# Seven-product groups for the first token half of a feed-forward layer too

## The chip, the cores and the metric

The program runs on one core of a Trainium2 chip. The metric is the device time of one execution in microseconds; lower is better. The kernel before takes 2988.46 us, the median of 3 runs (2985.38 to 2988.88). PE is the matrix engine (TensorE), DVE the vector engine, ACT the scalar engine, POOL the general engine (GpSimd) and SP the engine that issues most of the transfers.

## The reference

One block of a diffusion transformer, on 2048 tokens of 1024 channels in fp32. The part after the state space scan, which is what the change touches, is this:

```
vb = silu(layernorm(depthwise_conv31(v * sigmoid(v2)) + dw_bias))
merged = sigmoid(g_a) * (ya @ w_proj_a) + sigmoid(g_b) * (vb @ w_proj_b)
x = x + g1 * (merged @ w_out)
h = rmsnorm(x, norm2_g) * (1 + sc2) + sh2
x = x + g2 * ((silu(h @ w_gate) * (h @ w_up)) @ w_down)      # hidden 2816
out = rmsnorm(x, norm_f_g)
```

The hidden width is 2816, which is 22 column tiles of 128. The convolution has 31 taps and runs over the tokens, channel by channel.

## The kernel before, in words

Matmuls at fp32 accuracy are made from three: each operand is split into a high and a low part (ACT writes the high part, DVE subtracts it to get the low part), and high·high, high·low and low·high are accumulated. A *product* here is four 128-row steps of contraction for 512 tokens of one column tile: 12 matmuls of 128x512.

The 2048 tokens go through the tail in two halves of 1024, one after the other. For the first half: `merge` (L1080), `out_proj` (L1099) in two pieces of 512 tokens, `h2` (L1124, the norm and modulation), `ffn` (L1148), `final` (L1599, transposes of the result, last norm, output). Then the same for the second half, whose `merge` begins beside the first half's `final`.

The two halves have different feed-forward code. The first half's `ffn` makes gate and up of a column tile by 96 matmuls (8 products for 1024 tokens and both matrices) and adds the down product to an accumulator in SBUF, by one DVE instruction per column tile of the result and chunk (L1191). The second half's `ffn_s` makes 20 of its 22 tiles in *groups* of seven products, 84 matmuls (`group`, L1415): it forms sums and differences of the weights on DVE (L1390 to L1397), uses sums of the activations that were prepared before, and puts the results together from PSUM by DVE and ACT (L1430, L1432, L1456, L1460, L1462). Its down product is scaled by ACT (L1526) and added to the array d_x1 in HBM by accumulating transfers that POOL issues (L1527). Its weights are staged as a list of jobs (`next_job`, L1358): converted three jobs ahead, sums formed five ahead, loaded seven ahead, with a ring of four raw tiles beside the pool's own two.

Background work is written as generators that are advanced from within the matmul loops. `tick` (L79) is called at every third matmul and adds a credit, RATE; a generator issues its next piece when there is credit, and `dve` subtracts what the foreground itself needs of DVE. `finish` (L112) issues whatever is left of a generator at once. The second half's convolution (`conv` L903: 29 DVE instructions per channel tile at L920, 232 in all; `conv_stat` L1024: the statistics, with 8 matmuls at L1047, a Newton iteration of 12 small DVE steps at L141 to L147, and `rstd_row`, whose matmuls at L973 each need a DVE tile from L971) runs in the background of the first half's `ffn`. `conv_apply` (L1056) follows it. `mod_rest` (DVE work at L347) is earlier background work beside the first half's `merge`.

Engines run their instructions in the order in which the program's scheduler puts them; tiles come from pools (16 slots each, four scratch buffers and two raw weight buffers and so on), and a tile waits for the last reader of the buffer it takes.

Of the kernel before, what the change touches and what calls it, by code (L numbers as in the profile page):

```python
# [28 lines left out]
RATE = (0.75, 0.65, 0.61, 0.53, 0.56)  # L29
# [11 lines left out]
GAP_L, GAP_V, GAP_R = 1440, 1792, 2016  # L41


class Kernel:
# [158 lines left out]
    def setup(self):  # L203
        tc, nc, A, ctx = self.tc, self.nc, self.A, self.ctx
        self.cp = ctx.enter_context(tc.tile_pool(name="const", bufs=1))
        self.small = ctx.enter_context(tc.tile_pool(name="small", bufs=2))
        self.gap("gapl", GAP_L)
# [694 lines left out]
    def conv(self, vp, ft, hf, csum):  # L902
# [3 lines left out]
        x = vp.tile([128, HALF + 30], F32, tag="cin", name=self.nm("cin"), bufs=2)  # L906
# [23 lines left out]
    def conv_edge(self, vp, csum):  # L930
# [3 lines left out]
        t = vp.tile([128, HALF + 30], F32, tag="cin", name=self.nm("edge"), bufs=2)  # L934
# [88 lines left out]
    def conv_stat(self, vp, hf, csum, res):  # L1023
# [10 lines left out]
        for k in range(8):  # L1034
            c = vp.tile([128, HALF + 30], F32, tag="cin", name=self.nm("cvs"), bufs=2)[:, 0:HALF]
# [19 lines left out]
    def conv_apply(self, vp, hf, S, st, res):  # L1055
# [4 lines left out]
        for k in range(8):  # L1060
            x = vp.tile([128, HALF + 30], F32, tag="cin", name=self.nm("cva"), bufs=2)[:, 0:HALF]
# [62 lines left out]
    def h2(self, hf, rs, S, res, c0=0, W=HALF):  # L1124
        nc = self.nc
        cs = slice(c0, c0 + W)
        ts = slice(hf * HALF + c0, hf * HALF + c0 + W)
        n = W // 128
        yield (4,)
        rstd = self.rstd_small(rs, n)  # L1130
        yield 1.5
        yield (4,)
        row = yield from self.rstd_row(rstd, n)
        if c0 == 0:
            res.append(([self.slot(S, name="h2h") for k in range(8)], [self.slot(S, name="h2l") for k in range(8)]))
        hh, hl = res[-1]
        for k in range(8):
            x = self.t4(name="x1t")[:, 0:W]
            nc.sync.dma_start(x, self.d_x1[k, :, ts])
            h, l = hh[k][:, cs], hl[k][:, cs]  # L1140
            s, b = self.s2[:, k : k + 1], self.mod2[:, 8 + k : 9 + k]
            nc.vector.tensor_tensor(x, x, row[:, 0:W], op=OP.mult)
            nc.scalar.activation(h, x, AF.Identity, scale=s, bias=b)
            nc.vector.tensor_scalar(x, x, s, b, op0=OP.mult, op1=OP.add)
            nc.vector.tensor_tensor(l, x, h.bitcast(F32), op=OP.subtract)  # L1145
            yield 3.0 * W / HALF

    def ffn(self, hf, h2, S, acc, cut0, rs=None):  # L1148


        nc, A = self.nc, self.A
        hs = slice(hf * HALF, (hf + 1) * HALF)
        hh, hl = h2
        for m in range(8):
            a = self.slot(S, F32, name="x1")
            acc.append(a)
        c0 = 0
        for cn in (2, 4, 4, 4, 4, 4):
            ah, al = [], []
            first, last = c0 == 0, c0 + cn == 22  # L1160
            for bl in ((0,), (1,)) if cut0 and first else ((0, 1),):
                cs = slice(bl[0] * 512, (bl[-1] + 1) * 512)
                for t in range(cn):
                    col = slice((c0 + t) * 128, (c0 + t + 1) * 128)
                    wg = self.wload(A["w_ffn_gate"][0, :, col])
                    pg = self.mm()
                    self.gemm(pg, wg, 0, hh, hl, blocks=bl)
                    g = self.t4(name="fg")[:, cs]
                    nc.scalar.activation(g, pg[:, cs], AF.Silu)
                    wu = self.wload(A["w_ffn_up"][0, :, col])  # L1170
                    pu = self.mm()
                    self.gemm(pu, wu, 0, hh, hl, blocks=bl)
                    if bl[0] == 0:
                        ah.append(self.slot(S, name="ah"))
                        al.append(self.slot(S, name="al"))
                    nc.vector.tensor_tensor(g, pu[:, cs], g, op=OP.mult)
                    self.split(g, ah[t][:, cs], al[t][:, cs])
                    self.dve(2.3)
                    yield "up"
            if first:  # L1180
                for m in range(8):
                    nc.sync.dma_start(acc[m], self.d_x1[m, :, hs])
            for bl in ((0,), (1,)) if rs and last else ((0, 1),):
                cs = slice(bl[0] * 512, (bl[-1] + 1) * 512)
                for m2 in range(4):
                    w = self.wload(A["w_ffn_down"][0, c0 * 128 : (c0 + cn) * 128, m2 * 256 : (m2 + 1) * 256])
                    for mm in range(2):
                        m = m2 * 2 + mm
                        ps = self.mm()
                        self.gemm(ps, w, mm * 128, ah, al, blocks=bl)  # L1190
# [121 lines left out]
    def stage(self, j, what):  # L1312
# [3 lines left out]
        elif what == "sums":  # L1316
            if j["sums"]:
                j["sums"]()
# [580 lines left out]
```

## Time and profile before

| | us |
|---|---|
| median of 3 runs | 2988.46 |
| the profiled execution | 2991.2 |
| its span | 2989.4 |
| PE busy in it | 2911.4 (97%) |
| DVE busy in it | 2087.4 (70%) |
| ACT, POOL busy in it | 1066.0 (36%), 238.4 (8%) |

The stretches of the tail in the trace are: first `merge` 1180 to 1276 us, first `out_proj` to 1375, first feed-forward to 2111, first `final` with the second `merge` to 2200, second `out_proj` to 2290, second feed-forward to 2976, the end. A row "L920 DVE SCALAR_TENSOR_TENSOR acc<-cin,dwk,acc ... x232 | 285.3, 1277 | 0.5" reads: 232 instructions of line 920, 285.3 us busy, 1277 ns each, 0.5 us of idle time in front of them. In the rows by stretch an engine's number is its busy time with its count of instructions in brackets, then come TensorE's granted clock as a share of full speed, the busy share of the transfer engines, and GB/s. The array d_x1 is "d_x" there.

### The profile page before, as it was taken

How to read it: one execution, taken by the hardware profiler on the slowest of the kernel's cores; microseconds unless marked ns; L12 is line 12 of the kernel's file. 1: busy time of each engine (PE TensorE's matmuls, PEld its weight loads, DVE VectorE, ACT ScalarE, POOL GpSimd, SP SyncE). 2: the span in 40 equal slices, each digit the busy share in tenths (PEclk: the TensorE clock that was granted, in tenths of full speed). 3: DMA queues.
4: the chain of work that ended last, by engine and by line, in shares of the span. 5: the costliest groups of instructions: out<-in, count | busy, mean ns of one | idle time of the engine just before them, and what ended most of it. 6: DMA issues, size and time to landing. Idle time of an engine off the chain costs nothing.

```text
span 2989.4 us, 34432 instructions
## 1 busy us (share of the span) xinstructions
PE 2911.4 (97%) x12987; PEld 2357.1 (79%) x12987; DVE 2087.4 (70%) x3118; ACT 1066.0 (36%) x1457; POOL 238.4 (8%) x393
## 2 busy tenths in 40 slices
PE   7999999999999989999999999999999999999999
PEld 3778778788888877877888888888787788888887
DVE  6389989997888477667787878865746744344446
ACT  4323345334343454233212121123324544444433
POOL 0111322100010000000000000000000001100110
PEclk8999999999999999999999999999999999999999
DMA  5344545534443467857222122233456555645544
GB/s 205 126 118 122 159 160 177 178 101 120 129 120 104 153 217 253 290 199 222 78 64 61 60 64 64 64 113 98 148 181 208 126 116 124 141 112 117 122 101 148
DMA packets 392807, 408.14 MB, mean 137 GB/s; under 512 B 33281, under 2 KB 326497, under 8 KB 392640
## 3 DMA queue, kind: packets, MB, share of 16 engines
q1 hardware_dynamic: 341696, 276.78, 29.9%
q0 software_dynamic: 37488, 124.41, 15.2%
q10 hardware_dynamic: 13456, 4.75, 0.7%
q8 instruction: 102, 1.67, 0.2%
q14 instruction: 65, 0.53, 0.1%
HBM read 280.42 MB, written 125.42 MB: 136 GB/s over the span
## 4 chain that ended last, share of the span: by engine, by line
issue 46%; PE 39%; DVE 6%; DMA 5%; POOL 2%; ACT 1%; ACTq 0%; POOLq 0%; DVEq 0%; SPq 0%
PE mm L1296 18%; PE mm L182 16%; DVE acc L920 2%; PE ms L1296 2%; DMA wm<-in_w_mod_dram 1%; PE ms L741 1%; DVE lo L162 1%; DMA d_xt<-xts 1%; DMA d_in<-st 1%; POOL d_x L1112 1%; PE ms L696 0%; DMA ma<-d_ma 0%; PE mm L312 0%; DMA Braw<-in_ssm_b_re_dram 0%; DMA dwr<-in_dw_kernel_dram 0%
## 5 line engine op out<-in xcount | busy, mean ns | idle before, releaser
L920 DVE SCALAR_TENSOR_TENSOR acc<-cin,dwk,acc 128x1009 f32<-128x1009 f32 (+1 forms) x464 | 570.2, 1270 | 1.1 <-ACT acc L916 0.5
L160 ACT ACTIVATE hi<-raw 128x1024 fp32r<-128x1024 f32 (+1 forms) x212 | 222.6, 1050 | 770.0 <-PE mm L182 714.0
L182 PE MATMUL mm<-hh,hi 128*128 128x512 f32 x1152 | 478.4, 415 | 0.5 <-ACT hh L446 0.5
L182 PE MATMUL mm<-hl,hi 128*128 128x512 f32 x1152 | 454.1, 394 | 0.0
L182 PE MATMUL mm<-hh,lo 128*128 128x512 f32 x1152 | 453.4, 394 | 0.0
L162 DVE TENSOR_TENSOR lo<-raw,hi 128x1024 fp32r<-128x1024 f32 (+1 forms) x212 | 256.2, 1208 | 91.8 <-ACT hi L160 91.1
L182 PE MATMUL mm<-h2h,hi 128*128 128x512 f32 x704 | 274.8, 391 | 0.0
L182 PE MATMUL mm<-h2l,hi 128*128 128x512 f32 x704 | 274.0, 389 | 0.1
L182 PE MATMUL mm<-h2h,lo 128*128 128x512 f32 x704 | 274.0, 389 | 0.0
L182 PEld LDWEIGHTS mm<-hh,hi 128*128 128x128 f32 x1152 | 217.8, 189 | 46.5 <-issue 2.2
L182 PEld LDWEIGHTS mm<-hh,lo 128*128 128x128 f32 x1152 | 217.3, 189 | 46.9 <-issue 0.4
L182 PEld LDWEIGHTS mm<-hl,hi 128*128 128x128 f32 x1152 | 218.1, 189 | 44.5 <-issue 1.4
L182 PEld LDWEIGHTS mm<-h2l,hi 128*128 128x128 f32 x704 | 132.2, 188 | 28.1 <-DVE h2l L1145 0.5
L182 PEld LDWEIGHTS mm<-h2h,hi 128*128 128x128 f32 x704 | 132.2, 188 | 27.6 <-issue 0.3
L182 PEld LDWEIGHTS mm<-h2h,lo 128*128 128x128 f32 x704 | 132.1, 188 | 27.3
L182 PE MATMUL mm<-al,hi 128*128 128x512 f32 x352 | 136.8, 390 | 0.0
L182 PE MATMUL mm<-ah,hi 128*128 128x512 f32 x352 | 136.7, 391 | 0.0
L182 PE MATMUL mm<-ah,lo 128*128 128x512 f32 x352 | 136.6, 389 | 0.0
L182 PE MATMUL mm<-mgh,hi 128*128 128x512 f32 x256 | 101.7, 398 | 4.5 <-DVE xt L1111 3.3
L1337 DVE TENSOR_TENSOR l<-wx,h 128x1024 fp32r<-128x1024 f32 x40 | 48.9, 1223 | 81.0 <-ACT h L1334 81.0
L182 PE MATMUL mm<-vbh,hi 128*128 128x512 f32 x256 | 101.2, 395 | 0.9 <-DVE o L1610 0.9
L182 PE MATMUL mm<-mgl,hi 128*128 128x512 f32 x256 | 100.8, 394 | 0.9 <-DVE mgl L195 0.9
(540 smaller groups left out, 5749.8 us busy)
## 6 DMA issues: line engine op xcount, KB each, us to landing
raw<-in_w_in_dram SPq DMA_DIRECT2D x72, 512.0 KB
d_x<-fd POOLq DMA_DIRECT2D x72, 512.0 KB, 8.4
wm<-in_w_mod_dram SPq DMA_DIRECT2D x48, 512.0 KB
d_g<-gsig POOLq DMA_DIRECT2D x32, 512.0 KB, 4.3
raw<-in_w_out_dram SPq DMA_DIRECT2D x32, 512.0 KB
raw<-in_w_ffn_gate_dram SPq DMA_DIRECT2D x28, 512.0 KB
raw<-in_w_ffn_up_dram SPq DMA_DIRECT2D x28, 512.0 KB
wd<-in_w_ffn_down_dram SPq DMA_DIRECT2D x26, 512.0 KB
```

Source lines behind the costliest of these rows:

```text
L160: nc.scalar.activation(hi, raw, AF.Copy)
L162: nc.vector.tensor_tensor(lo, raw, hi.bitcast(F32), op=OP.subtract)
L182: nc.tensor.matmul(ps[:, b * bw : (b + 1) * bw], wt[:, k, c0 : c0 + 128], mv[k][:, b * bw : (b + 1) * bw], start=(k == 0 and j == 0), stop ...
L741: nc.tensor.matmul(ps.rearrange("p (i m) -> p m i", i=8), IN[:, d, i, :], rhs, start=True, stop=True)
L920: self.behind(nc.vector.scalar_tensor_tensor(t, x[:, i : i + W], K(i), t, op0=OP.mult, op1=OP.add), LAG)
L1112: nc.gpsimd.dma_start(self.d_x1[m, :, ts], xt)
L1296: nc.tensor.matmul(ps, wt[:, k, c0 : c0 + 128], mv[k], start=start and k == 0 and j == passes[0], stop=stop and k == n - 1 and j == passes ...
L1337: i = nc.vector.tensor_tensor(lo, f, hi.bitcast(F32), op=OP.subtract)
```

## The change

The first half's feed-forward uses `ffn_s` too; `ffn`, `h2` and the job list are gone. Two of its 22 column tiles, and the first down product, stay plain. Weights of all groups, of both halves, are now staged by `prep`, one *unit* ahead (a unit is a group or a pair of down loads): there are three raw tiles F, three pairs of split tiles R and one half-size pair R4, and the unit after next is loaded at the end of the current one.

```diff
-RATE = (0.75, 0.65, 0.61, 0.53, 0.56)
+RATE = (0.75, 0.65, 0.62, 0.6, 0.6)
...
+    def prep(self, u, what):
...
+            if what == "load":
+                nc.sync.dma_start(kc(F[2]), up)
+                nc.sync.dma_start(kc(F[0][:, L], 4), gate[:, 0:4])
+                nc.sync.dma_start(kc(F[1][:, R], 4), gate[:, 4:8])
+            elif what == "sums":
+                TT(F[0][:, R], F[2][:, L], F[2][:, R], op=OP.add)
+                TT(F[1][:, L], F[0][:, R], F[0][:, L], op=OP.subtract)
+                TT(F[2][:, L], F[0][:, L], F[2][:, L], op=OP.subtract)
+            elif what == "last":
+                TT(F[1][:, R], F[1][:, R], F[1][:, L], op=OP.subtract)
+                u["S4"] = self.conv_parts(F[1][:, R], self.R4, 4)
+            else:
+                n = {"a": 0, "b": 1, "c": 2}[what]
+                u[what] = self.conv_parts(F[n], self.R[u["R"][n]], 8)
...
+        for i, u in enumerate(units):
+            v, w = nxt(i + 1), nxt(i + 2)
...
+                plan = (["sums"], ["a"], ["b"], ["last"], ["c"]) if isg else ([], ["a"], ["b"], [], [])
+                def ahead(n):
+                    for what in plan[n]:
+                        self.prep(v, what)
+                    if n == 4:
+                        self.prep(w, "load")
+                self.group(u, X, a[u["t"] % 2 + (2 if u["t"] >= 20 else 0)], ahead)
```

The first half's down product so goes through ACT and the accumulating transfers (L1460 of the changed kernel) instead of the accumulator in SBUF, and `final_first` reads its result back from d_x1:

```diff
+    def final_first(self, vp):
...
+        for j in range(9):
+            if j < 8:
+                xs.append(self.spare(vp, 1).rearrange("p (k t) -> p k t", k=8))
+                nc.gpsimd.dma_start(xs[j], self.d_x1[:, :, j * 128 : (j + 1) * 128].rearrange("k p t -> p k t"))
+            if j:
+                ps = self.mm()
+                for k in range(8):
+                    nc.tensor.transpose(ps[:, k * 128 : (k + 1) * 128], xs[j - 1][:, k, :], self.ident)
```

The second half's convolution is put behind `mod_rest`, in a pool of its own for its inputs, so that it may begin beside the second half's `proj_a` and the first `merge`; what is left of it is finished after the last group of the first half:

```diff
             em.append(self.bg(self.mod_rest(vp)))
+            em.append(self.bg(convolve()))
...
+        f0 = feed(0)
+        self.finish(em[1])
         self.rate = RATE[4]
         e = self.bg(self.conv_apply(vp, 1, "Q", st1, vb1))
         take(f0)
         self.finish(e)
-        e = self.bg(self.final(0, acc, 0, 8))
+        e = self.bg(self.final_first(vp))
```

`feed(hf)` is the sequence from `out_proj` to the last group, for either half. By count the changed program has 240 fewer matmuls of 128x512 (11444 for 11684), 38 fewer DVE scalar_tensor_tensor of 128x1024, 240 more DVE tensor_tensor of 128x512, 82 more ACT instructions of 128x1024 and 146 more of 128x512, 80 more accumulating transfers and 8 more loads on POOL.

Three places show how instructions move. The first is PE near the end of the first feed-forward, where the convolution's variance is turned into a row (dgr and onesm are its operands; h2h, h2l with hi, lo are gate and up of a later tile). Before:

```order
L973 MATMUL mm_14993<-dgr_14994,onesm 128x128
L973 MATMUL mm_14993<-dgr_14997,onesm 128x128
L182 MATMUL mm_14923<-h2h_10706,hi_14919 128x512
L973 MATMUL mm_14993<-dgr_15000,onesm 128x128
L973 MATMUL mm_14993<-dgr_15003,onesm 128x128
L182 MATMUL mm_14923<-h2l_10714,hi_14919 128x512
L973 MATMUL mm_14993<-dgr_15006,onesm 128x128
L973 MATMUL mm_14993<-dgr_15009,onesm 128x128
L182 MATMUL mm_14923<-h2h_10706,lo_14921 128x512
L973 MATMUL mm_14993<-dgr_15012,onesm 128x128
L973 MATMUL mm_14993<-dgr_15015,onesm 128x128
```

After, right behind the last product of the last group (T4 with ex tiles); four more dgr matmuls follow before the next product, which is the last down unit's:

```order
L1218 MATMUL mm_15240<-T4h_11632,ex_11468 128x512
L1218 MATMUL mm_15240<-T4l_11634,ex_11468 128x512
L1218 MATMUL mm_15240<-T4h_11632,ex_11469 128x512
L1048 MATMUL ms_15367<-onesm,vs_15023 128x1 x8
L974 MATMUL mm_15391<-dgr_15392,onesm 128x128
L974 MATMUL mm_15391<-dgr_15395,onesm 128x128
L974 MATMUL mm_15391<-dgr_15398,onesm 128x128
L974 MATMUL mm_15391<-dgr_15401,onesm 128x128
```

What stood in pairs between the products of a column tile stands in a block by itself between a group and a down unit.

The second is POOL at the end of the first feed-forward. Before, stores of the convolution (d_cv) were followed by the outputs of `final`:

```order
L927 DMA d_cv<-acc_13454 128x1024
L927 DMA d_cv<-acc_13896 128x1024
L927 DMA d_cv<-acc_14283 128x1024
L1612 DMA out_dram<-o_15556 128x1024
L1612 DMA out_dram<-o_15641 128x1024
L1612 DMA out_dram<-o_15694 128x1024
L1612 DMA out_dram<-o_15779 128x1024
```

After, the last accumulating stores (fd) stand ahead of the loads of the transposes' inputs (ex), which read what they add to:

```order
L1460 DMA d_x_95<-fd_15640 128x1024
L1460 DMA d_x_95<-fd_15711 128x1024
L1460 DMA d_x_95<-fd_15714 128x1024
L1538 DMA ex_15744<-d_x_95 128x8x128
L1538 DMA ex_15758<-d_x_95 128x8x128
L1538 DMA ex_15801<-d_x_95 128x8x128
L1538 DMA ex_15873<-d_x_95 128x8x128
L1548 DMA out_dram<-o_15769 128x1024
```

The loads have come in between, and the first of them waits for all the accumulating stores.

The third is DVE in the middle of the first feed-forward. Before, one tile's up (fg from mm) and the low parts of weights (lo) and of activations (al) stand among the convolution (acc from cin):

```order
L920 SCALAR_TENSOR_TENSOR acc_11300<-cin_11296,dwk,acc_11300 128x1024
L162 TENSOR_TENSOR lo_11672<-raw_11668,hi_11670 128x1024
L920 SCALAR_TENSOR_TENSOR acc_11299<-cin_11296,dwk,acc_11299 128x1024
L920 SCALAR_TENSOR_TENSOR acc_11300<-cin_11296,dwk,acc_11300 128x1024
L1176 TENSOR_TENSOR fg_11600<-mm_11608,fg_11600 128x1024
L162 TENSOR_TENSOR lo_11734<-raw_11730,hi_11732 128x1024
L920 SCALAR_TENSOR_TENSOR acc_11299<-cin_11296,dwk,acc_11299 128x1024
L195 TENSOR_TENSOR al_11664<-fg_11600,ah_11663 128x1024
```

After, one stretch of a group: sums of weights (raw and ex tiles of 512), what puts the products together (fg and fu, from ms and mm), and low parts:

```order
L1280 TENSOR_TENSOR raw_11470<-ex_11472 128x512
L923 TENSOR_TENSOR acc_12045<-acc_12045,acc_12046 128x1024
L1281 TENSOR_TENSOR raw_11471<-raw_11470 128x512
L927 TENSOR_TENSOR cs_8672<-cs_8672,acc_12045 128x1024
L1282 TENSOR_TENSOR ex_11472<-raw_11470,ex_11472 128x512
L921 SCALAR_TENSOR_TENSOR acc_12550<-cin_12547,dwk,acc_12550 128x1024
L1313 TENSOR_TENSOR fg_12470<-ms_12469,fg_12470 128x512
L912 MEMSET cin_13114 128x15
L1313 TENSOR_TENSOR fu_12471<-mm_12467,fu_12471 128x512
L1256 TENSOR_TENSOR lo_11465<-raw_11470,hi_11464 128x1024
L1256 TENSOR_TENSOR lo_11467<-raw_11471,hi_11466 128x1024
```

One channel tile of the convolution ends here (L923, L927) and the next begins; short steps that wait for the weights' loads, for PE and for each other stand between.

## Rows read from the trace of the kernel before

**Rows 1.** Busy time of each engine, matmuls, clock and DMA share by stretch

```profile
1180.00:1276.00 96.00, 95.12 (x450) 79.17 (x448) 64.67 (x57) 17.52 (x17) 1.06 (x2) 1.00 0.88 299
1276.00:1375.00 99.00, 94.23 (x404) 75.59 (x405) 61.96 (x91) 33.62 (x41) 8.15 (x15) 0.97 0.60 197
1375.00:2111.00 736.00, 735.93 (x3254) 605.96 (x3253) 557.60 (x524) 171.73 (x170) 4.81 (x9) 1.00 0.27 84
2111.00:2200.00 89.00, 85.34 (x403) 70.93 (x402) 57.25 (x132) 23.42 (x30) 4.26 (x8) 0.98 0.53 181
2200.00:2290.00 90.00, 89.37 (x399) 72.95 (x398) 52.34 (x76) 36.46 (x47) 7.57 (x14) 1.00 0.58 185
2290.00:2976.00 686.00, 680.05 (x3011) 558.20 (x3010) 339.40 (x484) 293.52 (x362) 68.41 (x86) 1.00 0.53 125
```

**Rows 2.** Waits of PE from 1180 us to the end: total, times, longest (us)

```profile
PE mm L182 <- DVE xt L1111: 3.3, 3, 1.7
PE mm L1605 <- DVE ny L147: 2.8, 1, 2.8
PE mm L1296 <- ACT fg L1430: 1.7, 1, 1.7
...
```

**Rows 3.** The same columns as Rows 1, 100 us of each feed-forward half

```profile
1500.00:1600.00 100.00, 100.00 (x442) 82.49 (x441) 77.36 (x66) 16.97 (x16) 0.54 (x1) 1.00 0.19 59
2400.00:2500.00 100.00, 100.00 (x441) 82.25 (x440) 40.48 (x50) 43.10 (x50) 13.66 (x16) 1.00 0.64 137
```

**Rows 4.** DVE by line and shape, 1375 to 2111 us: busy, mean, idle before

```profile
L920 DVE SCALAR_TENSOR_TENSOR acc<-cin,dwk,acc 128x1024 f32<-128x1024 f32 x232 | 285.3, 1277 | 0.5
L162 DVE TENSOR_TENSOR lo<-raw,hi 128x1024 fp32r<-128x1024 f32 x69 | 84.0, 1218 | 18.9 <-ACT hi L160 18.4
L1191 DVE SCALAR_TENSOR_TENSOR x<-mm,mod,x 128x1024 f32<-128x1024 f32 x48 | 61.4, 1280 | 34.3 <-PE mm L182 33.9
L1176 DVE TENSOR_TENSOR fg<-mm,fg 128x1024 f32<-128x1024 f32 x20 | 24.5, 1223 | 86.7 <-PE mm L182 86.7
```

**Rows 5.** DVE and ACT by line and shape, 2345 to 2930 us, same columns

```profile
L1337 DVE TENSOR_TENSOR l<-wx,h 128x1024 fp32r<-128x1024 f32 x40 | 48.9, 1223 | 81.0 <-ACT h L1334 81.0
L1432 DVE TENSOR_TENSOR fg<-ms,fg 128x512 f32<-128x512 f32 x20 | 13.8, 690 | 61.6 <-PE ms L1296 61.6
L1390 DVE TENSOR_TENSOR wx<-wu 128x512 f32<-128x512 f32 x20 | 13.7, 685 | 8.9 <-DMA wu<-in_w_ffn_up_dram 8.9
...
L1526 ACT ACTIVATE fd<-mm,mod 128x1024 f32<-128x1024 f32 x72 | 79.1, 1111 | 62.7 <-PE mm L1296 35.3 <-DMA d_x<-fd 24.6 <-DVE T4l L195 2.8
```

**Rows 6.** Timeline of the convolution's statistics (PE) and of one Newton (DVE)

```profile
2015.26 1.84 PE L1047 MATMUL ms<-onesm,vs 128*128 128x1 f32 x16
...
2023.91 0.61 PE L973 MATMUL mm<-dgr,onesm 128*128 128x128 f32 x4
...
2026.41 0.71 PE L973 MATMUL mm<-dgr,onesm 128*128 128x128 f32 x4
...
2113.38 0.15 DVE L141 TENSOR_SCALAR nv<-ssf 128x1 f32<-128x1 f32 x1 [7.08 <-ACT o L1608]
...
2115.77 1.28 DVE L1610 SCALAR_TENSOR_TENSOR o<-mm,ny,gf 128x1024 f32<-128x1024 f32 x1
```

**Rows 7.** Accumulating stores (the page) and the reloads of x, issue to landing

```profile
d_x<-fd POOLq DMA_DIRECT2D x72, 512.0 KB, 8.4
...
DMA to landing us min/median/max: 3.3/8.2/11.9
```

**Rows 8.** PE after the first half's last transposes, and a window after

```profile
2156.36 1.06 PE L1605 MATMUL mm<-ident,x 128*128 128x128 f32 x8 [2.76 <-DVE ny L147]
2158.33 0.76 PE L182 MATMUL mm<-vbh,hi 128*128 128x512 f32 x1 [0.91 <-DVE o L1610]
...
2158.00:2162.00 4.00, 3.67 (x10) 2.95 (x11) 1.96 (x3) 1.64 (x2) 0.53 (x1) 0.61 0.84 294
```

More of the change, by code (lines that the diff above doesn't have):

```diff
@@ L1121, in out_proj @@
         res.append(rs)
[L1124 to L1190, printed above, removed]
-                        nc.vector.scalar_tensor_tensor(acc[m][:, cs], ps[:, cs], self.mod2[:, 24 + m : 25 + m], acc[m][:, cs], op0=OP.mult, op1=OP.add)
-                        if rs and last and bl[0]:
-                            sq = rs[0] if m == 0 else self.t4(shape=(128, 512), name="sq")
-                            nc.scalar.activation(sq, acc[m][:, cs], AF.Square)
-                            if m:
-                                nc.vector.tensor_tensor(rs[0], rs[0], sq, op=OP.add)
-                        self.dve()
-                        yield "down"
-            c0 += cn
@@ L1407, in down_jobs, with spare @@
-    def down_jobs(self, ring, c0, cn):
-        n = 1024 // cn
-        def load(i):
-            raw = self.wp.tile([128, cn, n], F32, tag="raw", name=self.nm("wd"))
-            self.nc.sync.dma_start(raw, self.A["w_ffn_down"][0, c0 * 128 : (c0 + cn) * 128, i * n : (i + 1) * n].rearrange("(k p) c -> p k c", p=128))
-            return raw
-        return [self.job((cn, n), ring["w"], lambda i=i: load(i)) for i in range(cn)]
-    def group(self, J, X, a):
+    def spare(self, vp, n, dt=F32):
+        if n < 3:
+            return self.ex.tile([128, HALF], dt, tag="ex", name=self.nm("ex"))
+        return vp.tile([128, HALF], dt, tag="csum", name=self.nm("ex"))
@@ new lines, in weights_open @@
+    def weights_open(self, vp):
+        R = []
+        for n in range(3):
+            if n < 2:
+                R.append([self.wp.tile([128, HALF], F32R, tag=t, name=self.nm(t)) for t in ("hi", "lo")])
+            else:
+                R.append([self.spare(vp, 0, F32R), self.spare(vp, 1, F32R)])
+        self.R = R
+        self.F = [self.wp.tile([128, HALF], F32, tag="raw", name=self.nm("raw")) for _ in range(2)] + [self.spare(vp, 2)]
+        t = self.spare(vp, 3, F32R)
+        self.R4 = [t[:, 0:512], t[:, 512:1024]]
+        self.last_act = self.last_dve = None
@@ L1504, in ffn_s @@
+        units = []
+        grp = lambda t: units.append({"kind": "group", "t": t})
+        dwn = lambda c0, cn, cols, b=(0, 1): units.append({"kind": "down", "c0": c0, "cn": cn, "cols": cols, "blk": b})
         for c in range(9):
             if c:
-                for t in (2 * c, 2 * c + 1):
-                    groups[t] = self.group_jobs(ring, t)
-            downs[c] = self.down_jobs(ring, 2 * c, 2)
+                grp(2 * c)
+                grp(2 * c + 1)
+            dwn(2 * c, 2, (0, 1))
@@ L1542, in ffn_s @@
[L1542 to L1559 removed]
+            grp(t)
@@ new lines, in ffn_s @@
+        for b in ((0,), (1,)) if rs is not None else ((0, 1),):
+            dwn(18, 4, (0, 1), b)
+            dwn(18, 4, (2, 3), b)
+        order = [0, 1, 2]
+        for u in units:
+            n = 3 if u["kind"] == "group" else 2
+            u["R"] = order[0:n]
+            order = order[n:] + order[0:n]
+        nxt = lambda i: units[i] if i < len(units) else None
+        self.prep(units[0], "load")
+        self.prep(units[0], "a")
+        self.prep(units[0], "b")
+        self.prep(units[1], "load")
@@ L1828, in tail @@
         take(c1)
[L1829 to L1851 removed]
+        rs, end = [], []
+        f1 = feed(1, rs, end)
+        take(f1, 2)
         acc = end[0]
```

378 lines of the change are left out of this document (164 added, 214 removed).

## The prediction, as it was put on record

> **What bounds the kernel now.** I read the table by stretch first. In the first feed-forward, 1375 to 2111 us, PE is busy 735.93 of 736.00 us at a granted clock of 1.00, while DVE is busy 557.60, ACT 171.73 and the transfers 0.27 [rows 1]. So that stretch is as long as its matmuls, and one matmul less there is worth its distance to the next. That distance is 100/441 = 0.2268 us [rows 3]: the second half, which already has the groups, runs at the same 441 per 100 us. The reader is to see in rows 3 that 50 DVE and 50 ACT instructions with transfers at 0.64 do not slow PE there. Rows 1 also show what the form is worth: the second half's stretch is 686 us, the first's 736. The other stretches of the tail lose little: PE is idle 0.9 of 96 us in the first merge, 4.8 of 99 in the first out_proj and 3.7 of 89 in the first final with the second merge [rows 1]. The list of PE's waits [rows 2] names what these are: output tiles of out_proj, one Newton, a group's activation; the longest are 2.8 and 1.7 us. New waits will not hide behind anything, because PE has no slack.
>
> **1. The matmuls that go.** 20 column tiles of the first half fall from 96 to 84 matmuls: 240 x 0.2268 = 54.4 us. All are on the path, since DVE's and ACT's work lay beside them. This term is -54.4.
>
> **2. DVE in the first feed-forward.** Per tile, before: two low parts of 1.22, the up of 1.22, the activations' low part of 1.22 and 61.4/20 = 3.1 for the accumulation, together 8.0 us [rows 4]. After: five combinations of 512 at 0.69, one low part of activations at 1.22, four sums at 0.69, three low parts at 1.22 and a half one at 0.69: 11.8 us [rows 5]. For 20 tiles that is +76 us. By order, some 40 of the 232 convolution steps now stand before this stretch: -40 x 1.28 = -51 us [rows 4]. DVE is then busy 558 + 76 - 51 = 583 of 736 - 54 = 682 us, 85%, with 99 us of idle time where it had 178. Its work still fits, but each instruction waits in its order: the third order piece has three sums, of which the first waits for a load that is issued only when the raw tile has been read, then what frees PSUM for PE. I followed one cycle of two groups and a down unit through DVE's order with these durations: PE had to wait for nothing, with 1.6 us to spare at the closest place (the combination before the last product). I take +3 us for cycles that fall less well. The bounds: nothing if all fit; +15 if a third of the 20 groups, 7, lose 2.2 us each, which lies between the waits of 0.91 and 2.76 us in [rows 8].
>
> **3. The convolution's statistics at the end of the groups.** Before, the eight dgr steps lie between products, four pairs from 2023.91 to 2026.41 + 0.71 [rows 6], 3.2 us. After, by the first order piece, PE does onesm with vs (1.84 us, needed before too), waits for a Newton (2113.38 to 2115.77, 2.4 us [rows 6]) in which DVE's order also has two low parts of 1.22, so 4.8, and for the dgr steps, 3.2, of which about half is matmul time that was there before. The idle time is about 4.8 + 1.6 = 6.4 us. Behind a wait of this length the clock falls: after 2.76 + 0.91 us of idle time the window 2158 to 2162 was granted 0.61, and held 10 matmuls where 17.6 fit, 1.7 us lost [rows 8]. The sum is +8; from 4 (DVE's low parts come later than I think) to 12 (the activation's row adds its own latency).
>
> **4. The start of the second merge.** Before, `final` transposes from SBUF. After, the first transposes stand about 40 matmuls (9.1 us) behind the last down product, in the second order piece behind 80 accumulating stores on POOL: the last product needs its scaling on ACT (1.1 [rows 5]), its accumulating store (8.4 [rows 7]) and a load of 512 B pieces, for which the nearest rows are the reloads with 3.3 at least and 8.2 median [rows 7]; I take 4.5, near the low end, since only this one is awaited. Sum 14.0 + issue 0.3, against 9.1: 5.2 us of stall. A second one, for PSUM behind the first output's Newton (2.4) and scaling (1.28 [rows 6]), comes to 2; smaller ones and the clock to 3. Before had 3.7 here [rows 1] and lost about 1.7 to the clock [rows 8], less what stays. Net +6, from 2 to 12 (the load at 8.2, and `conv_apply` late as well).
>
> **5. The first merge and out_proj.** 16 convolution steps now stand among the first merge's DVE instructions: 64.67 + 16 x 1.28 = 85 of 96 us [rows 1, 4], with transfers at 0.88 that must now bring the convolution's inputs too. `mod_rest` is pushed on to the start of out_proj. I take +4, from 0 to 12, near out_proj's present idle time of 4.8 us.
>
> **6. The start of the first groups.** The second half's out_proj and what follows it waits for a group's activation and a combination (1.7 us the longest, [rows 2]); the first half now has this form: +2, from 0 to 5.
>
> **7. The second half's weights.** Its staging goes from seven jobs ahead to one unit. A group lasts 84 x 0.2268 = 19.05 us, and the DVE there has half its time free (339 of 686 [rows 1]); loads cost it 8.9 us of idle time over 20 groups [rows 5], none of which is PE's. I take 0, from -3 (the present start of the groups waits for loads) to +8.
>
> **8. The end.** By order, the last transposes now stand behind all products; their output needs a Newton and a scaling, 2.4 + 1.28 [rows 6], which nothing covers: +4, from 0 to 5.
>
> Sum: -54.4 + 3 + 8 + 6 + 4 + 2 + 0 + 4 = -27.4. The profiled execution took 2991.2 us (span 2989.4), so it would take 2963.8; it lies 2.7 above the median of the runs, so the forecast is 2961 us. The terms' own bounds do not all fall on one side, so its own range is 2946 to 2976.
>
> **Rivals.** *The whole gain.* If the scheduler's order leaves no wait of these (terms 3 to 5 a third as large, the rest nothing): -54.4 + 6 - 2.7 from 2991.2, 2940 us. For it: the first half's statistics have room in the background, and 99 us of DVE's time are free. Against it: the dgr block and the dependence of the transposes on the last store are in the order itself.
>
> *DVE becomes the bound in the first feed-forward.* The mechanism: DVE waits at the head of its order for a weight's load or for a product, and the combinations that PE needs are behind it. Its price is each microsecond of DVE idle time beyond the 99 that it has. With as many as before, 178 (736 - 558, [rows 1]), PE loses 79: 2961 - 3 + 79 = 3037 us. It is slower than before from 27.4 + 3 + 6 = 36 us of such loss on, that is, DVE idle for over 135 us. For it: 86.7 and 34.3 us of DVE's present idle time are waits for PE of this very kind [rows 4], and the load ahead is shallower. Against it: those waits exist because DVE is ahead of PE; in the second half, where DVE waits 61.6 us for one combination alone [rows 5], PE does not wait. The Trainium skill, page TensorE: Matmul & The Clock Gate, section HAM oscillation — how this bites in real kernels, describes a kernel in which brief idle times between matmul groups make the clock go back and forth; by that rule short waits in each group would cost more than their length. Rows 3 hold the clock at 1.00 in the second half's groups, so the trace agrees only where there is a wait, as in rows 8.
>
> *The weights come late in both halves.* With one unit of lookahead, a load issued at the end of a unit lands after its sums are due, at a price of about the 0.91 us of a short wait [rows 8], say 1, in each of 40 groups: 2961 + 40 = 3001 us, or 2961 + 20 = 2981 where it affects one half only. For it: the third raw tile is free only when the current unit's c part is converted. Against it: transfers at 0.27 and 0.53 [rows 1] leave room, and the reloads in rows 7 land in 3.3 to 8.2 us, less than half of a group.
>
> **How the numbers follow.** The forecast 0.60, the whole gain 0.17, weights late 0.11 (half of it still faster by over 0.2%, mostly in the first half alone), DVE the bound 0.12 (a third of it not slower). What a measurement of this kernel can tell from no change is 0.2%, 6 us. Faster: 0.60 + 0.17 + 0.06 + 0.02 = 0.85. Same: 0.03 + 0.02 = 0.05. Slower: the rest, 0.10. The range of 8 in 10 reaches from 2937, below the whole gain, to 2984, where the late weights begin.
>
> **What would show it.** Right: PE idle for 5 to 8 us in one piece before the last down unit of the first half, with dgr tiles behind it; a wait of the transposes for a load from d_x after it; 100-us windows of the first feed-forward with 441 matmuls and DVE at 85%. Wrong: windows with fewer than 430 matmuls and waits of PE for combinations in every group (DVE the bound), waits of sums for weight loads in both halves (weights late), or no wait in the two places (the whole gain). A stall of the first merge above 12 us would break term 5.

## The result: 2.3% slower, and the profile after

The changed kernel takes 3057.24 us, the median of 4 runs (3053.82 to 3062.02), against 2988.67 us before: a ratio of 1.0231, 95% interval 1.0212 to 1.0250. The forecast was 2961 us, with the sign wrong. The profiled execution has a span of 3060.3 us. Below are its stretches, cut at the first product of each stage as in [rows 1]: length, busy time of PE, weight loads, DVE, ACT and POOL with counts, granted clock, transfers' busy share, GB/s.

```profile
1185.00:1279.00 94.00, 93.29 (x433) 77.47 (x434) 83.96 (x75) 17.45 (x18) 1.60 (x3) 1.00 0.79 266
1279.00:1380.00 101.00, 93.16 (x418) 75.08 (x417) 76.60 (x99) 38.80 (x48) 8.10 (x15) 1.00 0.71 227
1380.00:2135.00 755.00, 698.71 (x2979) 568.76 (x2978) 595.65 (x670) 329.34 (x388) 71.14 (x87) 0.96 0.53 127
2135.00:2247.00 112.00, 99.26 (x452) 81.26 (x452) 62.49 (x138) 28.93 (x36) 13.36 (x18) 0.95 0.66 205
2247.00:2338.00 91.00, 89.42 (x398) 72.82 (x397) 54.62 (x79) 36.56 (x48) 8.12 (x15) 1.00 0.61 193
2338.00:3053.00 715.00, 691.90 (x3049) 568.65 (x3048) 338.63 (x496) 294.38 (x364) 68.02 (x85) 0.99 0.51 119
```

The reader is to see three things. The first feed-forward is 755.6 us long although 240 matmuls are gone: cut in the same way it was 728.7 before, so it lost 26.9 and, without the 54.4 that the matmuls gave, 81 us. The second feed-forward, whose matmuls are the same as before, went from 688.7 to 714.9 (up to PE's last matmul). And the second merge with the transposes went from 99.6 to 111.3. PE's clock is below 1.00 in just these stretches. The list of PE's waits from 1180 us on (engine and line that waited, what for; total, times, longest, in us) names the places:

```profile
PE mm L1218 <- DVE fu L1313: 37.8, 15, 4.1
PE mm L1218 <- ACT fg L1310: 20.2, 3, 8.1
PE mm L1542 <- DMA ex<-d_x: 8.4, 1, 8.4
PE mm L1218 <- ACT ex L1175: 6.3, 1, 6.3
PE mm L1218 <- ACT fd L1459: 5.6, 3, 3.1
PE mm L974 <- DVE dgr L972: 5.0, 2, 4.8
```

The first row is one wait in most cycles (a cycle is two groups and a down unit), six in the first half and nine in the second: at the last product T4 of the first group behind a down unit. This is one of them in the timeline of the second half (start, length, engine, line; in brackets the idle time before and what ended it): ACT's and DVE's conversion that frees the raw tile, the load's issue on SP, DVE and then PE:

```profile
2540.14 1.06 ACT L1253 ACTIVATE ex<-ex 128x1024 fp32r<-128x1024 f32 x1 [1.33 <-PE mm L1218]
2541.23 1.23 DVE L1256 TENSOR_TENSOR ex<-ex,ex 128x1024 fp32r<-128x1024 f32 x1 [6.62 <-ACT ex L1253]
2542.48 0.37 SPq L1276 DMA_DIRECT2D ex<-in_w_ffn_up_dram  x1
...
2552.05 0.69 DVE L1280 TENSOR_TENSOR raw<-ex 128x512 f32<-128x512 f32 x1 [9.59 <-DMA ex<-in_w_ffn_up_dram]
2552.77 0.69 DVE L1281 TENSOR_TENSOR raw<-raw 128x512 f32<-128x512 f32 x1
2553.38 0.69 DVE L1282 TENSOR_TENSOR ex<-raw,ex 128x512 f32<-128x512 f32 x1
2553.98 0.69 DVE L1313 TENSOR_TENSOR fg<-ms,fg 128x512 f32<-128x512 f32 x1
...
2556.32 1.23 DVE L1256 TENSOR_TENSOR lo<-raw,hi 128x1024 fp32r<-128x1024 f32 x1 [1.65 <-ACT hi L1253]
2557.46 0.68 DVE L1313 TENSOR_TENSOR fu<-mm,fu 128x512 f32<-128x512 f32 x1
...
2558.20 0.50 PE L1218 MATMUL mm<-T4h,ex 128*128 128x512 f32 x1 [1.55 <-DVE fu L1313]
```

Read it from the end. T4 waits for DVE's combination fu, which frees its PSUM tile. On DVE, fu stands behind the next group's first low part (which waits for ACT), behind fg, and behind the next group's three sums. The first sum waits 9.59 us for a load and starts 9.6 us after that load's issue at 2542.48. The load could not be issued sooner: its raw tile is free only when the current group's part c is converted (the low part that DVE ended at 2542.46), and that needs the split pair that the down unit has just given up (ACT waits 1.33 us for PE there). Eight such loads of the second half, from 2478 to 2921 us, take 9.6 to 10.6 us from issue to the sum. The window of transfers from 2543 to 2551 us shows what runs beside this one (queue: packets, MB, share of the 16 transfer engines):

```profile
q0 software_dynamic: 349, 1.24, 77.6%
q1 hardware_dynamic: 1081, 0.54, 25.6%
```

q0 carries the down unit's accumulating stores, q1 the weight. That the stores make the load slow is tested below. In the second half alone (2400 to 2950 us) DVE stood still for such loads for 92.5 us:

```profile
L1280 DVE TENSOR_TENSOR raw<-ex 128x512 f32<-128x512 f32 x18 | 12.4, 689 | 92.5 <-DMA ex<-in_w_ffn_up_dram 92.5
```

The row of before that answers to it is L1390 in [rows 5], with 8.9 us.

The second row of PE's waits, three in the first half, has other causes, on ACT. This is ACT before the one of 7.6 us at 1546 us:

```profile
1533.79 1.10 ACT L1459 ACTIVATE fd<-mm,mod 128x1024 f32<-128x1024 f32 x1
1544.25 1.24 ACT L917 ACTIVATE acc<-cin,vec,dwk 128x1024 f32<-128x1024 f32 x1 [9.37 <-DMA cin<-d_vp]
1545.40 0.58 ACT L1310 ACTIVATE fg<-mm 128x512 f32<-128x512 f32 x1
```

The group's first copy fg (L1310), which PE's T2 needs, stands behind the first step of a new channel tile of the convolution (L917), and that waits for its input. Before the third wait, at 1874 us, the same step waits 6.44 us for the convolution's store. Before the longest, 8.1 us at 1477 us, the copy fg itself waits 5.87 us for an accumulating store to give up a scratch buffer.

### The profile page after: what moved, and what is told of

Same layout as the page of the kernel before. It is cut to its first block, busy times and chain, and to the rows that moved or that the text cites. A ratio compares the mean times of both kernels' runs of the same rounds, so it can differ in the third digit from the quotient of the medians.

```text
span 3060.3 us, 34722 instructions
## 1 busy us (share of the span) xinstructions
PE 2893.6 (95%) x12747; PEld 2334.3 (76%) x12747; DVE 2165.3 (71%) x3296; ACT 1234.7 (40%) x1687; POOL 313.0 (10%) x480
## 4 chain that ended last, share of the span: by engine, by line
issue 42%; PE 40%; DMA 7%; DVE 6%; POOL 3%; ACT 1%; ACTq 0%; POOLq 0%; DVEq 0%; SPq 0%
PE mm L182 20%; PE mm L1218 15%; DMA ex<-in_w_ffn_up_dram 2%; DVE acc L921 2%; POOL d_x L1460 2%; PE ms L1218 1%; PE ms L742 1%; DVE lo L162 1%; DMA d_x<-fd 1%; DMA x1t<-d_x 0%; PE ms L697 0%; DMA d_in<-st 0%; DMA dwr<-in_dw_kernel_dram 0%; ACT hi L1253 0%; DMA wm<-in_w_mod_dram 0%
## 5 line engine op out<-in xcount | busy, mean ns | idle before, releaser
L160 ACT ACTIVATE hi<-raw 128x1024 fp32r<-128x1024 f32 x148 | 156.4, 1056 | 293.0 <-PE mm L182 245.3
L1460 POOL DMA_DIRECT2D d_x<-fd x152 | 129.0, 849 | 1139.3 <-ACT fd L1459 1115.2
L162 DVE TENSOR_TENSOR lo<-raw,hi 128x1024 fp32r<-128x1024 f32 x148 | 180.3, 1219 | 80.2 <-ACT hi L160 79.7
L1459 ACT ACTIVATE fd<-mm,mod 128x1024 f32<-128x1024 f32 x152 | 166.6, 1111 | 135.3 <-PE mm L1218 99.8
L1218 PE MATMUL mm<-ah,hi 128*128 128x512 f32 x480 | 188.4, 393 | 2.3 <-ACT fd L1459 2.3
L1218 PE MATMUL mm<-ah,lo 128*128 128x512 f32 x480 | 187.4, 391 | 0.0
L1310 ACT ACTIVATE fg<-fg 128x512 f32<-128x512 f32 x80 | 50.5, 632 | 288.2 <-DVE fg L1313 274.2
L1256 DVE TENSOR_TENSOR lo<-raw,hi 128x1024 fp32r<-128x1024 f32 x89 | 108.2, 1219 | 71.8 <-ACT hi L1253 71.8
L1218 PE MATMUL mm<-ah,ex 128*128 128x512 f32 x448 | 138.6, 391 | 1.2 <-ACT ah L1310 1.0
L1256 DVE TENSOR_TENSOR ex<-raw,ex 128x1024 fp32r<-128x1024 f32 (+1 forms) x79 | 75.0, 949 | 61.2 <-ACT ex L1253 61.1
L1218 PEld LDWEIGHTS mm<-ah,hi 128*128 128x128 f32 x480 | 90.6, 189 | 22.6 <-ACT fd L1459 3.1
L1218 PEld LDWEIGHTS mm<-ah,lo 128*128 128x128 f32 x480 | 90.6, 189 | 19.0
```

The costliest lines, as they stand in the source:

```text
L160: nc.scalar.activation(hi, raw, AF.Copy)
L162: nc.vector.tensor_tensor(lo, raw, hi.bitcast(F32), op=OP.subtract)
L1218: nc.tensor.matmul(ps, wt[:, k, c0 : c0 + 128], mv[k], start=start and k == 0 and j == passes[0], stop=stop and k == n - 1 and j == passes ...
L1256: i = nc.vector.tensor_tensor(lo, f, hi.bitcast(F32), op=OP.subtract)
L1310: self.last_act = nc.scalar.activation(o, i, f)
L1459: nc.scalar.activation(o, ps, AF.Copy, scale=mod)
```

## The experiments

Each kernel ran beside the kernel before on the same chip. Lengths of stretches are from the profiled executions, from the first product of one stage to that of the next; a profiled execution can lie some 10 us from its kernel's median.

**Stores left out.** This kernel leaves out the down units' accumulating stores, except those of each half's first down unit. The edit, on the changed kernel:

```diff
+                            if u["c0"] == 0:
-                            nc.gpsimd.dma_start(self.d_x1[r, :, hs], o, accum_op=OP.add)
+                                nc.gpsimd.dma_start(self.d_x1[r, :, hs], o, accum_op=OP.add)
```

> This kernel leaves out the accumulating stores of the down product in both halves, except those of each half's first down unit; everything else stays. Theory (late weights): the loads for the group behind a down unit start only when PE leaves that unit, the accumulating stores stretch them to 9 us and more, and DVE's sums, which wait for them, stand ahead of the combination that the group's last product T4 needs. Without stores the loads land in 3 to 5 us, the waits before T4 (2.3 to 4.5 us, one in each cycle of both halves) fall below 0.5, the first half's feed-forward goes from 756 to 700-710 us, the second's from 715 to 688-693, the total to about 2975-2990. Rival 1 (DVE has too much to do beside the convolution): the first half stays at 740 or more, the second at 710. Rival 2 (the lookahead alone is too short, whatever the stores do): waits of 1.5 us or more stay before T4 in each cycle of both halves, total 3035 or more.

2968.34 us, ratio 0.993 (0.991 to 0.995): 89 us less than the changed kernel, and below the 2975 to 2990 expected. The first half's feed-forward (the first half, from here on) is 707.6 us, the second half's 686.3. The 500 us from 2400 us on, in the changed kernel and then in this one (columns as above):

```profile
2400.00:2900.00 500.00, 481.07 (x2076) 394.34 (x2075) 203.38 (x251) 204.50 (x242) 52.60 (x62) 0.98 0.53 116
```

```profile
2400.00:2900.00 500.00, 500.00 (x2208) 414.01 (x2207) 212.77 (x259) 210.34 (x252) 4.27 (x8) 1.00 0.20 62
```

DVE and ACT do the same work per group; only the transfers' share is less, and PE does not wait. This is the load that answers to the one at 2542 us above, and the sum that waits for it:

```profile
2528.72 0.37 SPq L1276 DMA_DIRECT2D ex<-in_w_ffn_up_dram  x1
...
2532.30 0.69 DVE L1280 TENSOR_TENSOR raw<-ex 128x512 f32<-128x512 f32 x1 [3.61 <-DMA ex<-in_w_ffn_up_dram]
```

It takes 3.6 us where it took 9.6, and the seven others from 2409 to 2828 us take as long. The one wait for fu that is left stands behind the second half's first down unit, whose stores remain; there the load takes 7.5 us:

```profile
2355.29 0.69 DVE L1280 TENSOR_TENSOR raw<-ex 128x512 f32<-128x512 f32 x1 [7.50 <-DMA ex<-in_w_ffn_up_dram]
...
2361.44 0.50 PE L1218 MATMUL mm<-T4h,hi 128*128 128x512 f32 x1 [2.18 <-DVE fu L1313]
```

Rival 2 falls: one unit of lookahead is enough when the loads have the transfer engines to themselves. Rival 1 falls with it. Whether a longer lookahead beside the stores would do the same wasn't tried.

**Order alone.** The loads and stores stay; the sums go behind the combination that T4 needs, and the conversions that follow them go back with them.

```diff
-                TT(F[0][:, R], F[2][:, L], F[2][:, R], op=OP.add)
+                i = TT(F[0][:, R], F[2][:, L], F[2][:, R], op=OP.add)
+                if behind:
+                    self.order(i, self.last_dve)
...
-                plan = (["sums"], ["a"], ["b"], ["last"], ["c"]) if isg else ([], ["a"], ["b"], [], [])
+                plan = ([], [], ["sums", "a"], ["b"], ["last", "c"]) if isg else ([], ["a"], ["b"], [], [])
...
-                        self.prep(v, what)
+                        self.prep(v, what, True)
```

> Order alone: the three sums for the next group are put behind the combination that T4 needs, and the conversions that follow them move one product later; loads and stores stay as they are. Late weights held ahead in DVE's order: the waits before T4 go from 2.3-4.5 to under 0.7 us in both halves, second half 715 to about 692, first half 756 to about 725, total about 3000-3010. Rival 1 (DVE has too much to do): nothing changes in either half, 3045-3060. Rival 2 (lookahead too short): the wait moves from T4 to the first product of the next group, whose weights now come later; total 3050-3070.

3000.52 us, ratio 1.0030 (1.0013 to 1.0047): 57 us less than the changed kernel. The second half is back at 688.0, the first at 726.6. In the list of PE's waits from 1375 us on, the wait for DVE's fu is gone (its five largest rows):

```profile
PE mm L1218 <- ACT fg L1312: 19.4, 3, 8.7
PE mm L1544 <- DMA ex<-d_x: 9.7, 1, 9.7
PE mm L1218 <- ACT ex L1175: 6.8, 1, 6.8
PE mm L1218 <- ACT fd L1461: 6.0, 2, 3.1
PE mm L974 <- DVE dgr L972: 5.0, 2, 4.8
```

The same 500 us as above hold 2208 matmuls here too, with the transfers as busy as in the changed kernel (0.55 for 0.53):

```profile
2400.00:2900.00 500.00, 500.00 (x2208) 414.01 (x2207) 207.57 (x255) 214.10 (x250) 54.36 (x64) 1.00 0.55 120
```

So the place in DVE's order decides. The two runs together say that a late load and an order that puts it ahead of what PE needs are both necessary for the wait.

**Fewer taps.** `range(2, 31)` becomes `range(2, 9 if hf else 31)` in `conv`.

> This kernel leaves out 22 of the 29 DVE steps of each channel tile of the second half's convolution (176 of 232 steps, 225 us of DVE). Rival 1 (DVE has too much to do): the first half's feed-forward goes from 756 to 690 or less, the total to 2990 or less. Late weights: the waits before T4 stay in each of the first half's cycles, at the 2.3 to 3.0 us that the second half shows without any convolution; the first half comes to 715-735, the total to 3020-3040. Rival 2: as late weights.

3055.45 us, ratio 1.0221 (1.0201 to 1.0242): no gain. The first half is 746.6 us, 9 less than in the changed kernel, where 715 to 735 was expected. DVE's share in 1640 to 2100 us is 204 of 460 us (366 of 440 in the same cycles of the changed kernel), and PE waits for the same combination six times, up to 2.5 us, as the second half does:

```profile
1640.00:2100.00 460.00, 447.41 (x1952) 367.86 (x1952) 204.25 (x248) 195.74 (x229) 41.59 (x49) 0.99 0.49 112
```

```profile
PE mm L1218 <- DVE fu L1313: 12.6, 6, 2.5
```

DVE's amount of work is not what makes these waits; at most it lengthens them, since in the same cycles of the changed kernel they reach 4.1 us. My own expectation of 3020 to 3040 failed as well: the waits in the cycles shrank, but others grew where the short convolution now reached its statistics, in the middle of the first groups (a pitch is the distance between the starts of two matmuls; here 8.8 us at 1608 us and 5.9 at 1624), and the second half's stayed.

**The convolution's inputs, first attempt.** The load of the next channel tile is written in front of the current tile's DVE steps:

```diff
...
+        if hf and ft < 7:
+            self.cin_next = self.cin_load(ft + 1, hf)
         for i in range(2, 31):
...
```

> The load of the convolution's next channel tile is issued one channel tile ahead, so that ACT's first step on it does not wait for it with a group's copies behind. Late weights and heads of order: the waits of T2 for ACT of 8.0 and 4.9 us (where ACT stands at the convolution's first step) and part of the loads' contention go, 10 to 18 us, total about 3040-3047. Rival 1: DVE is as busy as before, no change (within 4 us). Rival 2: no change.

3058.08 us, ratio 1.0234 (1.0215 to 1.0253): nothing, where 3040 to 3047 was expected. The trace says why: the scheduler moves ACT's first step on the next tile up with it, right behind the load, so that ACT still stands there (9.5 us for cin at 1538, 6.0 for the store of acc at 1866).

**Late transposes.** On the kernel with the sums behind, the eight bf loads of `h2s_second` move out of its loop to stand in front of it, and `yield (4,)` in `final_first` becomes `yield (4 if j else 30,)`.

> On the kernel with the sums behind: the first half's transposes start 30 steps (about 20 us) later beside the second merge, and the eight reloads of the first half's second 512 tokens (bf) are issued together instead of two at a time between the weights' loads. Theory (waits for transfers at the head of an order): the transposes' wait of 9.7 us and what follows it go, second merge 110 to about 98 us; the wait of 7 us at 1400 us for the activations goes or falls under 3; total 3000 to about 2980-2985. Rival (the transfers themselves lack bandwidth there): the waits stay within 2 us of their sizes wherever the transposes stand, 2995-3002.

2994.39 us, ratio 1.0022 (1.0008 to 1.0037), nearer to the rival's 2995 than to the 2980 to 2985 expected. The bf loads did what was expected (PE's wait of 6.8 us for their tiles became two of 1.4 and 1.0). The transposes did not: the second merge is longer, 118.1 for 109.7. The first transposes wait for nothing now, but the seventh and eighth wait 5.94 and 1.59 us for their own loads at 2162 and 2165 us, and the sixth 2.25 us for DVE's scaling of an output: `finish` pushes the same eight into less time, and in POOL's timeline the eighth load is issued only when the sixth transposes have ended. The wait was moved, not removed.

**A higher rate.** `RATE[3]` from 0.6 to 0.7 on top of that.

> As the one with late transposes, and the convolution is issued faster beside the groups (0.7 for 0.6), so that its statistics come between the products of a group and nothing is left for the end. Theory: the wait of 5.07 us for dgr and the slower clock behind it go, 5 to 8 us less than with late transposes, 2973-2980; DVE has room for it. Rival (DVE near its limit beside the groups): combinations come late in the groups, first half's feed-forward 5 us or more longer, 2985 or more.

3036.65 us, ratio 1.0153 (1.0132 to 1.0174): 42 us worse. The first half goes from 721.9 to 757.0. In 1440 to 1900 us DVE is busy 411 of 460 us, where it was 384, and PE waits for conversions (the largest rows from 1440 to 2140 us; hi, lo and ex are conversions):

```profile
PE mm L1220 <- ACT fg L1314: 13.6, 3, 6.7
PE ms L1220 <- ACT hi L1255: 6.9, 4, 2.3
PE mm L1220 <- DVE fu L1317: 6.0, 1, 6.0
PE mm L1220 <- DVE lo L1258: 6.0, 6, 2.8
PE ms L1220 <- ACT ex L1255: 4.4, 2, 2.3
```

So the rival about DVE near its limit forecast this outcome. A likely reading is that with the sums late the conversions behind them have little room when DVE is 89% busy; no run separates DVE's amount of work here from the order that the higher rate gives.

**The convolution behind.** As above, the rate 0.75, and `yield (20,)` in front of ACT's two steps of each channel tile.

> As the one with late transposes, the rate 0.75, and ACT's first two steps on a channel tile of the convolution come 20 steps (14 us) behind its load and behind the store of the tile before. Theory: the waits of a group's first copies on ACT of 7.5 and 4.0 us, where ACT stands at the convolution's first step for a load or a store, go: the first half's feed-forward another 10 to 15 us shorter than with the rate alone, total 2962-2970, below the kernel before. Rival: the convolution, with its pauses, doesn't end in time, and what is left of it stands on PE's path at the end, 2985 or more.

3018.53 us, ratio 1.0094 (1.0072 to 1.0115), not the 2962 to 2970 expected. The first half is 735.9 us, 21 less than at the rate 0.7. PE's waits for the copy fg fell from 13.6 us to 4.3, those for conversions stayed (6.5 us for ACT's hi in four waits), and the longest one for dgr is 8.1 us (6.9 at the rate 0.7). It doesn't tell the theory from the rate's harm.

**The convolution's inputs, second attempt.** On the kernel with the sums behind, at the rate 0.6, with the bf loads together and the transposes where the change has them. The input comes one channel tile ahead through ACT's queue, ACT's first step on a tile is held behind the last copy of the group in which it is written, and the sum of the tile goes to the other buffer:

```diff
...
+            nc.scalar.dma_start(x[:, 0 : HALF + 15], self.d_vp[ft, :, HALF - 15 : N])
...
-        nc.scalar.activation(a, x[:, 0:W], AF.Identity, scale=K(0), bias=self.V("dw_bias", ft))
+        i = nc.scalar.activation(a, x[:, 0:W], AF.Identity, scale=K(0), bias=self.V("dw_bias", ft))
+        if hf and self.last_act:
+            self.order(i, self.last_act)
...
+        if hf and ft < 7:
+            self.cin_next = self.cin_load(ft + 1, hf)
...
-        nc.vector.tensor_tensor(a, a, b, op=OP.add)
+        nc.vector.tensor_tensor(b, a, b, op=OP.add)
+        a = b
```

> The kernel with the sums behind, the eight reloads (bf) together, the transposes where they were, and three edits to the second half's convolution at the old rate 0.6: its input is loaded one channel tile ahead through ACT's own transfer queue, ACT's first step on a tile is held behind the last copy of the group in which it is written (the scheduler had moved it far ahead, where it waits for load or store), and the sum goes to the buffer that is reused later. Theory (waits at the heads of orders): the waits of T2 for ACT of 8.0 and 4.3 us go, the one of 8.5 us at 1460 us stays, the second merge stays at 110; first half's feed-forward 722 to 705-710, total about 2977-2985, at or below the kernel before. Rival: ACT's transfers hold up its copies, and the waits move to other products of the groups, 2995 or more.

2976.58 us, ratio 0.9956 (0.9939 to 0.9973): 14 us faster than the kernel before. The first half is 703.1 us, and the largest of PE's waits from 1375 us on are

```profile
PE mm L1233 <- ACT fg L1327: 9.2, 1, 9.2
PE mm L1559 <- DMA ex<-d_x: 7.3, 1, 7.3
PE mm L987 <- DVE dgr L985: 4.8, 1, 4.8
```

Which of the three edits to the convolution did most wasn't tried.

**The second attempt without the stores of each half's first down unit** (`if u["c0"]:` in front of the accumulating store).

> The kernel with the convolution's inputs ahead, and the accumulating stores of each half's first down unit left out (16 of 152). Theory (the four scratch buffers are held by stores of 8 to 9 us each, and a group's first copy needs one): the wait of 9.6 us for ACT in front of the second group's T2 at 1460 us goes, with the slower clock behind it, 8 to 12 us, about 2966. Rival (that wait comes from the activations' sums T4 or from ACT's other work): the wait stays above 5 us.

2964.19 us, ratio 0.9911 (0.9882 to 0.9939); the first half is 688.9 us and the wait of 9.2 us is gone. So that wait hangs on the stores, which hold the four scratch buffers; it is the one at 1477 us in the changed kernel.

**The convolution's edits without the sums.** The second attempt with the sums where the change has them.

> The changed kernel with the eight reloads together and the three edits to the convolution, and the sums where the change has them. If the two causes are separate: the waits before T4 stay in both halves (second half 714), the waits of T2 for ACT go, total 3057 less 15 to 22, about 3035-3042. If the convolution's place was what made DVE's sums late: the first half's waits before T4 shrink too, 3020 or less.

3051.15 us, the middle of two executions (3045.45 and 3056.84), ratio 1.0201 (1.0153 to 1.0249), not the 3035 to 3042 expected: PE waits 52.9 us for fu, 17 times, up to 6.1, where it was 37.8, and 8.5 us for fg, where it was 20.2. What goes from the waits on ACT comes back at T4, as long as DVE's order holds. The convolution's edits and the bf loads together were worth 24 us once the sums stood behind (3000.52 to 2976.58).

**Small steps on the second attempt**: rate 0.62, transposes 14 steps later.

> As the one with the convolution's inputs ahead, with the rate 0.62 for 0.6, so that the statistics come between products, and the first half's transposes 14 steps (10 us) later. Theory: the wait of 5 us for dgr goes and about half of the transposes' 9.7 us, 2968-2978. Rival (the convolution at a higher rate gets in between weights and combinations, as at 0.7): first half's feed-forward 10 us or more longer than with the inputs ahead.

2972.67 us, ratio 0.9942 (0.9923 to 0.9960), the fastest with the whole computation. The wait for dgr is gone, that of the transposes is 5.8 us; a pitch of 9.8 us at 1953 us is new. The difference to the kernel that it builds on lies within their runs' spread.

## Why the prediction was wrong, step by step

By the stretches of the two profiled executions, the changed kernel's span is 71 us longer, where -27.4 was forecast: -54.4 for the matmuls, +81.3 in the first half's feed-forward (steps 2, 3 and 6), +11.7 in the second merge (step 4), +0.3 in the first merge and out_proj (step 5), +26.2 in the second half's feed-forward (steps 7 and 8), and 6 elsewhere, most of it ahead of the first merge, where nothing was looked into. Steps 2 and 7 failed most.

- **Step 1** held: 240 matmuls less. Without stores the 500 us from 2400 us on hold 2208 matmuls, 0.2264 us each.
- **Step 2** failed. Its sum for DVE's busy time came out (583 us forecast, 596 measured). But it followed one cycle through DVE's order with DVE's durations, found 1.6 us to spare, and gave no duration to the load that the first sum waits for; the loads took over 9 us from issue to sum (9.3 to 12.7 in the first half's cycles from 1605 us on) because the accumulating stores, now in this half too, had most of the transfer engines (without them the second half's took 3.6). The first half's waits and slower matmuls, without the wait for dgr of step 3, came to 77 us (pitches over 0.5 us: 58; matmuls at 0.26 to 0.5: 18.5), of which step 6's are part; +3 was taken, +15 the bound. The waits for fu alone are 20.1 us, six waits of up to 4.1 us, where the bound had seven of 2.2; the two waits on ACT behind the convolution's first step, 7.6 and 4.5 us, were in no term.
- **Step 7** failed most clearly: 0 was taken, +8 the bound, 26 measured (688.7 to 714.9). I read [rows 5] as a load cost that is none of PE's; but that row was measured with the loads issued seven jobs ahead. The row says what loads cost at that lead, not at the new one, and the reloads of [rows 7], 8.2 us in the median beside such stores, were the nearest row for that.
- **Step 6**: +2 taken, up to 5. The window 1380 to 1480 us holds 338 matmuls where 441 fit, so 103 x 0.227 = 23 us are lost there, most of it in three pitches: 6.7 us for bf loads issued late, 2.7, and 8.5 for a scratch buffer; the rest is slower matmuls. The first half's down stores and SP's order were not counted in it.
- **Step 3** held: PE stands 4.8 us for dgr; 8 with the clock was taken, from 4 on.
- **Step 4** held in mechanism, with the size short: PE waits 8.4 us for the first load, and the stretch is 11.7 longer, +6 taken, up to 12. The term that was short is the last scaling on ACT, 1.1 taken: it ends 8.1 us after the last down product, because ACT's order has steps of `conv_apply` in front that wait for DVE. The store then took 8.1 us and the load 5.4, near the 8.4 and 4.5 taken. ACT's order there:

```profile
2138.25 1.25 ACT L1070 ACTIVATE vbh<-cva,vec 128x1024 fp32r<-128x1024 f32 x1 [3.50 <-DVE cva L1069]
...
2142.47 1.10 ACT L1459 ACTIVATE fd<-mm,mod 128x1024 f32<-128x1024 f32 x1
```

- **Step 5** was too dear: the first merge took 93.9 us (95.7 before), out_proj 100.8 (98.7), though DVE is at 84 of 94 us as worked out.
- **Step 8** was wrong: with the sums behind, the second half with the end takes 688.0 us, as before.

Of the rivals, *the weights come late in both halves* named the lookahead, the sums and both halves, with a chance of 0.11. Its price, 1 us in each of 40 groups, is close to the 37.8 us that PE waited for fu (fewer waits, each longer). What it lacks is the slower matmuls behind the waits (11 us in the second half; 18.5 in the first, behind all its waits) and the waits on ACT, so its 3001 us is short as well. *DVE becomes the bound* has in its mechanism the sentence that the runs bear out, that DVE waits at the head of its order for a weight's load with the combinations that PE needs behind it. But it put this in the first half alone and priced it by DVE's idle time, while the second half, with DVE busy 339 of 715 us, lost 26 us. That its 3037 us is the nearest figure is luck: by its own price the 160 us that DVE was idle in the first half would make 3019. The prediction's signs of being wrong came for both rivals: 395 matmuls per 100 us in the first half, waits of PE for combinations in most cycles, and waits of the sums for weight loads in both halves.

## What to carry to other kernels

A row in which a load costs nothing holds for the lead at which it was issued: when a change shortens the lead, time the load beside what will run with it (here 9.6 to 10.6 us beside accumulating stores in the second half, 3.6 without them), and ask what stands behind it on the engine that waits. An engine at half load can still hold up the bound; what counts is which instruction is at the head of its order. Putting one wait behind the result that PE needs gave back 57 us with the same loads and stores.

## What was not expected of the hardware

A 512 KB weight load took 9.6 us from issue to the instruction that waited for it while accumulating stores held 72 to 78% of the transfer engines' time, and 3.6 us with the stores left out; DVE's idle time for these loads in the second half fell from 92.5 to 43.8 us, and PE had one wait behind them, of 2.2 us, in place of nine. Short waits also cost more than their length: in the changed kernel's second half the gaps of over 0.5 us between the starts of matmuls come to 25.3 us, and the matmuls at 0.26 to 0.5 us (for 0.227) to another 11.3 us, at a granted clock of 0.98 to 0.99 where it was 1.00. Not every wait lowered it: from 2560 to 2562 us, behind the wait of 1.55 us, it was 1.00; from 2495 to 2498 us, behind one of 2.34 us, it was 0.50.
